# A fourth attention unit of each layer is turned by a DMA transpose: its words laid apart by GpSimd, joined one step later, its value products one step later

## The chip, the cores and the metric

The kernel runs on one core of one Trainium2 chip. The metric is device time in microseconds. Before the change the median of three runs is 1626.21 us (1625.96 to 1626.82).

## The reference, cut to what matters

A decoder trunk of two layers runs over 512 tokens of width 1024, all in float32. Each layer is a SwiGLU block, a mixing block and a second SwiGLU block. The mixing block holds the attention that the change touches:

```
z = rms_norm(x) @ W_in -> q (8 heads of 64), k, v (2 heads of 64), conv_B, conv_C, conv_h
scores = q @ k^T / 8 + ALiBi bias      window of 128: each block of 128 queries sees
                                       its own block of keys and the one before
p   = exp(scores - m) / (sum + exp(sink - m))
att = p @ v                            per head
y   = conv_B * depthwise_conv3(conv_C * conv_h)
x   = x + concat([att, y]) @ W_out
```

## The kernel before, in words

**Products.** Every matrix product is made of three TensorE passes over float32r halves: a number is split into a high part and the rest, and hi·hi, hi·lo and lo·hi are summed. A weight block is therefore loaded ("raw", 512 KB, line 210), cast on ScalarE to "wh", and subtracted on VectorE to "wl" (both line 228). The block `need_split` keeps two such splits ahead of TensorE. One group of 24 matmuls (lines 318, 319, 321) makes one 128 by 512 result "acc".

**The mixing block as steps.** `mix` runs the 18 groups of W_in in a fixed order. After the groups that make the queries and the convolution's inputs, a function `attend(step)` puts in a piece of attention: steps 6 to 17 each follow one group (`go_on`). A step's group and pieces stand in one instruction stream per engine. A planner orders each stream by the order of the program and by when it thinks that operands are ready, and the chip then works through each stream strictly in order.

**Attention units.** There are eight units, numbered 0 to 7: four blocks of 128 queries for each of two key heads, with four query heads in each. Unit 5 is block 1 of the second key head, unit 6 block 2, unit 7 block 3. A unit passes through three stages, at the steps that three tables name (`SCORES_AT`, `TURN_AT`, `VALUES_AT`):

- `scores`: matmuls of q and k, the maximum on VectorE (line 1558), the exponential on ScalarE (1575), the division on VectorE (1583). The result "p" (128 by 4 by 256, float32) lies in a buffer of the same eight that hold raw weight blocks.
- `turn`: p must stand the other way round for the product with v. In units 0, 2, 4, 6 and 7 TensorE transposes it in 128 by 128 blocks into PSUM ("pt", line 1616; eight blocks for units 2, 6 and 7). ScalarE then casts each half to "ph" (1621) and VectorE subtracts to get "pl" (1622).
- `values`: four matmuls with v into "o" (1633, 1634), a copy of the lower half on ScalarE ("ol", 1636) and two additions on VectorE into the attention output "m" (1639).

**Three units go another way.** `SEND_AT = {7: 1, 9: 3, 11: 5}` says that units 1, 3 and 5 are turned by DMA. `send` copies p on ScalarE so that the upper and the lower 16 bits of all words lie apart in a room called "crossing" (line 1590), and a DMA transpose from the queue of SyncE writes them, turned, back into p's buffer (1592). Two steps later `turn` calls `join` instead of the TensorE transposes: two ScalarE copies (line 1601) put the halves of the words together again, into the same room. The casts and subtractions follow as in the other units. The room has two places, used in turn: units 1 and 5 use the first, unit 3 the second.

**What sets the order around the change.** Three things. First, `attend` returns the last subtraction of the step's `turn`, and `go_on` then asks for the next weight splits under `tc.issue_after(last.ins)`: on VectorE the subtraction that makes "wl" may not stand ahead of that instruction. At step 14 the last instruction is that of unit 6, and two splits are asked for there. Second, the loads of W_out (ten blocks, four of them with a second load from GpSimd's queue that adds to the first, line 223) need raw buffers, and these come free when the units' p buffers and earlier splits are done with. Third, at step 17 the output projection begins (lines 827): its first chain "x_m" takes the tokens 0 to 255, and its third chain needs "ft2", sums over the tokens 0 to 511 that VectorE makes from m (lines 601, 602, then the split of line 228). GpSimd's own work here is two elementwise operations per convolution group (lines 1715, 1716) and the adding loads.

Of the kernel before, what the change touches and what calls it, by code (L numbers as in the profile page):

```python
# [54 lines left out]
STREAM_BACK_AT = {9: 0, 11: 1, 16: 2, 18: 3}  # L55
SCORES_AT = (5, 6, 7, 8, 9, 10, 12, 13)

SEND_AT = {7: 1, 9: 3, 11: 5}
TURN_AT = (6, 9, 8, 11, 10, 13, 14, 15)
VALUES_AT = (7, 10, 9, 12, 11, 14, 15, 16)  # L60
INSIDE = (11, 4, 5)
WARM = 3
XT_TAGS = ("sc", "aux", "aux", "mm", "sc", "sc", "aux", "aux")
# [12 lines left out]
def trunk_kernel(  # L76
# [23 lines left out]
    nc = tc.nc  # L100
# [34 lines left out]
    def words(ap):  # L135

        return ap.bitcast(U16).rearrange("p (n two) -> p two n", two=2)
# [1356 lines left out]
    def mix(l, norm, after):  # L1494
# [40 lines left out]
        class Unit:  # L1535
# [49 lines left out]
            def send(self):  # L1585


                self.room = crossing[:, todo.index(self) // 2 % 2, :]
                halves = self.room.bitcast(U16).rearrange("p (two n) -> p two n", two=2)
                nc.scalar.copy(halves, words(self.p.rearrange("p h k -> p (h k)")))  # L1590
                self.turned = self.p.rearrange("p h k -> p (h k)").bitcast(U16)
                nc.sync.dma_start_transpose(
                    self.turned.rearrange("p (c q) -> p c q", q=P),
                    halves.rearrange("p two n -> p (two n)"),
                )
# [11 lines left out]
            def turn(self):  # L1607

                self.pt = []
                for kb in range(self.lo // P, 2):  # L1610
                    if todo.index(self) in SEND_AT.values():
                        tp = self.join(kb)
# [30 lines left out]
        todo = [Unit(n, g) for g in range(NKV) for n in range(NT)]  # L1643
        crossing = g8(f"crossing_{l}", F32, (P, 2, 4 * 2 * P))

        def attend(step):

            done = None
            if step in SEND_AT:
                todo[SEND_AT[step]].send()  # L1650
            for at, stage in ((VALUES_AT, "values"), (TURN_AT, "turn"), (SCORES_AT, "scores")):
                if stage == "turn" and step + 1 == INSIDE[0]:
                    done = todo[VALUES_AT.index(step)].added
                    continue
                if step in at:
                    done = getattr(todo[at.index(step)], stage)() or done
            return done

        for j in range(NH // 2):
            acc = group(norm.h) if j else qacc  # L1660
            if j == 3:
                vv = take_values()
            qf = scaled(acc, f"qf_{l}_{j}", by=1.0 / 8.0)
            both = form(f"q_{l}_{j}", shape=(P, 2, S))
            qe, qo = both[:, 0, :], both[:, 1, :]
            nc.scalar.copy(qe[:HD, :], qf[:HD, :])
            nc.scalar.copy(qo[HD:, :], qf[HD:, :])
            nc.vector.tensor_sub(qe[HD:, :], qf[:HD, :], f32(qe[:HD, :]))
            nc.vector.tensor_sub(qo[:HD, :], qf[HD:, :], f32(qo[HD:, :]))
            q[2 * j], q[2 * j + 1] = qe, qo  # L1670
            attend(2 + j)
# [4 lines left out]
        step = 6  # L1676

        def product():

            def between(k, hi, lo):  # L1680
                if step == INSIDE[0] and k == INSIDE[2]:
                    todo[INSIDE[1]].turn()

            return group(norm.h, between, own=take_split(SPLIT_AHEAD - 1))

        def go_on():

            nonlocal step
            last = attend(step)
            if step == TURN_AT[-1]:  # L1690
                state["turned"] = last.ins
            step += 1
            with tc.issue_after(last.ins) if last else nullcontext():
                need_split(state["group"] - 1 + SPLIT_AHEAD + (step >= TURN_AT[-1]))

        for pair in range(2):
# [22 lines left out]
            for j in range(2):  # L1719
                last = nc.vector.tensor_mul(mixed[1][:, 2 * pair + j, :], product(), ys[j])  # L1720
# [64 lines left out]
```

## Time and profile before

| quantity | value |
|---|---|
| median of the runs shown | 1626.21 us |
| profiled execution: its time | 1626.19 us |
| profiled execution: its span | 1624.4 us |
| granted TensorE clock | 0.999 |
| TensorE matmul busy | 1615.4 us (99%) |
| VectorE busy | 1376.7 us (85%) |
| ScalarE busy | 1178.1 us (73%) |
| GpSimd busy | 216.5 us (13%) |

Shares are of the whole span. The steps that the change touches lie near 417 to 470 us in the first layer and near 1220 to 1273 us in the second, so a share over the span says little about them; the rows of those stretches do. "PE" is TensorE, "DVE" VectorE, "ACT" ScalarE, "POOL" GpSimd, and "SP" the queue of SyncE that issues most DMAs. In the lists by time a row gives start, duration, engine, line, operation and tiles, and in square brackets how long the engine had sat idle before and what ended that.

### The profile page before, as it was taken

Reading aid. Unit: us, or ns where it says so; the run is one execution under the profiler, and the core shown is the slowest. Engines: PE = TensorE matmul, PEld = TensorE weight load, DVE = VectorE, ACT = ScalarE, POOL = GpSimd, SP = SyncE. Lnnn points to the kernel's source line nnn. Section 1 sums busy time; section 2 is a strip of 40 time slices with the busy share of each in tenths; the row PEclk is TensorE's granted clock in tenths of the full one; section 3 lists DMA queues with packets and bytes.
Section 4 is the critical chain, followed back from the end, with each engine's and each line's share of the span. In section 5 each row is a group of like instructions: output and inputs, shape, how many; then the busy total and the mean of one; then the engine's idle time right before and its main releaser. Section 6 shows DMA issues by size and latency. Waiting matters only on the chain.

```text
span 1624.4 us, 21158 instructions
## 1 busy us (share of the span) xinstructions
PE 1615.4 (99%) x7571; PEld 1349.4 (83%) x7571; DVE 1376.7 (85%) x1788; ACT 1178.1 (73%) x1511; POOL 216.5 (13%) x191
## 2 busy tenths in 40 slices
PE   9999999999999999999999999999999999999998
PEld 7888888888898888888888888888888988888887
DVE  7978798988899977798998777989688998678997
ACT  6677777857766677778866777788586767878665
POOL 1211111001211111111011111110012111111121
PEclk9999999999999999999999999999999999999999
DMA  9999989822597698999767999998136978999892
GB/s 270 212 232 209 220 207 226 233 59 78 143 227 175 177 225 214 218 214 225 218 144 182 224 215 226 215 221 217 42 91 156 233 149 219 225 223 222 241 230 72
DMA packets 306031, 313.92 MB, mean 193 GB/s; under 512 B 125501, under 2 KB 188549, under 8 KB 305925
## 3 DMA queue, kind: packets, MB, share of 16 engines
q1 hardware_dynamic: 265412, 230.90, 50.1%
q0 software_dynamic: 40048, 81.27, 29.3%
q8 instruction: 59, 0.97, 0.2%
q14 instruction: 48, 0.39, 0.1%
q10 hardware_dynamic: 464, 0.40, 0.1%
HBM read 264.29 MB, written 2.10 MB: 164 GB/s over the span
## 4 chain that ended last, share of the span: by engine, by line
PE 98%; DVE 1%; DMA 0%; SPq 0%; issue 0%; ACT 0%; DVEq 0%
PE x L842 27%; PE y L842 13%; PE x_s L842 9%; PE acc L318 7%; PE acc L319 7%; PE acc L321 7%; PE w L842 7%; PE y_s L842 5%; PE x_m L827 3%; PE w_s L842 3%; PE y_m L827 1%; PE y_e L842 1%; PE acc L699 1%; PE x_e L842 1%; PE w_m L827 1%; PE sc L1555 0%
## 5 line engine op out<-in xcount | busy, mean ns | idle before, releaser
L228 DVE TENSOR_TENSOR wl<-raw,wh 128x1024 fp32r<-128x1024 f32 (+1 forms) x494 | 598.6, 1219 | 162.8 <-ACT wh L228 161.9
L228 ACT CAST wh<-raw 128x1024 fp32r<-128x1024 f32 (+1 forms) x494 | 514.1, 1044 | 304.6 <-PE x L842 92.8
L318 PE MATMUL acc<-xh,wh 128*128 128x512 f32 x392 | 153.3, 393 | 0.5 <-ACT wh L228 0.5
L319 PE MATMUL acc<-xl,wh 128*128 128x512 f32 x392 | 153.1, 391 | 0.0
L321 PE MATMUL acc<-xh,wl 128*128 128x512 f32 x384 | 149.7, 390 | 0.0
L223 POOL DMA_DIRECT2D raw<-in_ffn_wu_dram x40 | 50.6, 1272 | 381.6 <-DMA raw<-in_ffn_wu_dram 268.6
L318 PEld LDWEIGHTS acc<-xh,wh 128*128 128x128 f32 x392 | 73.8, 188 | 15.0 <-ACT wh L228 0.6
L319 PEld LDWEIGHTS acc<-xl,wh 128*128 128x128 f32 x392 | 73.7, 188 | 14.5
L321 PEld LDWEIGHTS acc<-xh,wl 128*128 128x128 f32 x384 | 72.1, 188 | 15.3
L223 POOL DMA_DIRECT2D raw<-in_ffn_wd_dram x34 | 41.0, 1218 | 272.0 <-DMA raw<-in_ffn_wd_dram 122.3
L223 POOL DMA_DIRECT2D raw<-in_ffn_wg_dram x40 | 49.1, 1237 | 201.9 <-DMA raw<-in_ffn_wu_dram 84.7
L269 DVE TENSOR_TENSOR raw<-raw,raw 128x1024 f32<-128x1024 f32 x58 | 70.5, 1220 | 1.7 <-DMA raw<-in_ffn_wu_dram 1.2
L1106 ACT COPY raw_a<-turned 128x1024 uint16<-128x1024 uint16 x48 | 63.5, 1357 | 0.0
L842 PE MATMUL x<-wl,ft1h 128*128 128x512 f32 x160 | 62.4, 390 | 0.0
L842 PE MATMUL w<-wh,fb21h 128*128 128x512 f32 x160 | 62.3, 390 | 0.0
L842 PE MATMUL y<-wh,ft3h 128*128 128x512 f32 x160 | 62.3, 390 | 0.0
L842 PE MATMUL x<-wh,ft1l 128*128 128x512 f32 x160 | 62.3, 389 | 0.0
L842 PE MATMUL x<-wl,ft2h 128*128 128x512 f32 x160 | 62.3, 389 | 0.0
L842 PE MATMUL x<-wh,ft2l 128*128 128x512 f32 x160 | 62.3, 389 | 0.0
L842 PE MATMUL x<-wh,ft1h 128*128 128x512 f32 x160 | 62.3, 389 | 0.0
L842 PE MATMUL w<-wh,fb21l 128*128 128x512 f32 x160 | 62.2, 389 | 0.0
L842 PE MATMUL y<-wh,ft3l 128*128 128x512 f32 x160 | 62.2, 389 | 0.0
(517 smaller groups left out, 4545.2 us busy)
## 6 DMA issues: line engine op xcount, KB each, us to landing
raw<-in_ffn_wu_dram SPq DMA_DIRECT2D x127, 512.0 KB, 5.6
raw<-in_ffn_wd_dram SPq DMA_DIRECT2D x105, 512.0 KB, 5.6
raw<-in_ffn_wg_dram SPq DMA_DIRECT2D x86, 512.0 KB, 5.3
raw<-in_ffn_wu_dram POOLq DMA_DIRECT2D x40, 512.0 KB, 9.1
raw<-in_ffn_wg_dram POOLq DMA_DIRECT2D x40, 512.0 KB, 6.5
raw<-in_w_in_dram SPq DMA_DIRECT2D x36, 512.0 KB, 4.0
raw<-in_ffn_wd_dram POOLq DMA_DIRECT2D x34, 512.0 KB, 8.2
raw<-in_w_out_dram SPq DMA_DIRECT2D x20, 512.0 KB, 4.6
```

Source lines behind the costliest of these rows:

```text
L223: nc.gpsimd.dma_start(out=r, in_=rows_of(*more), accum_op=ALU.add)
L228: return nc.scalar.copy(hi, raw), eng.tensor_sub(lo, raw, f32(hi))
L269: nc.vector.tensor_add(a11, a11, s1)
L318: nc.tensor.matmul(acc, hi[:, k, :], rhs[k][0], start=k == first, stop=False)
L319: nc.tensor.matmul(acc, hi[:, k, :], rhs[k][1], start=False, stop=False)
L321: nc.tensor.matmul(acc, lo[:, k, :], rhs[k][0], start=False, stop=k == last)
L699: nc.tensor.matmul(opening[n], (lo if part == "w" else hi)[:, k, :], xl if part == "x" else xh, start=n not in begun, stop=k == KC - 1 and ...
L827: nc.tensor.matmul(accs[c // 2][:, c % 2, :], w[:, k, cols], x_[:, 2 * h + k, :], start=start and c % 2 == 0 and h + k + i == 0, stop=h + ...
L842: nc.tensor.matmul(accs[u], x_[:, 2 * h + k, tok], w[:, k, :], start=start and h + k + i == 0, stop=h + k == 2 and i == 2, skip_group_chec ...
L1106: nc.scalar.copy(words(raws[self.b][:, c, :]), self.to[:, :, c, :])
```

## The change

Unit 6 joins the units that are turned by DMA. It is sent at step 13, and its `turn` stays at step 14, so one step lies between the two and not two. Its `values` move from step 15 to step 16, where unit 7's also are. The copy that lays its words apart is put on GpSimd (`IDLE_LAYS`), not on ScalarE. It uses the second place of the crossing room, after unit 3.

In `attend` a step may now hold several units of one stage, and the instruction that unit 6's `turn` returns is no longer handed on: at step 14 nothing is returned, so the two weight splits asked for there are no longer queued behind it.

```diff
-SEND_AT = {7: 1, 9: 3, 11: 5}
+SEND_AT = {7: 1, 9: 3, 11: 5, 13: 6}
 TURN_AT = (6, 9, 8, 11, 10, 13, 14, 15)
-VALUES_AT = (7, 10, 9, 12, 11, 14, 15, 16)
+VALUES_AT = (7, 10, 9, 12, 11, 14, 16, 16)
+IDLE_LAYS = (6,)
...
-                nc.scalar.copy(halves, words(self.p.rearrange("p h k -> p (h k)")))
+                lay = nc.gpsimd.tensor_copy if todo.index(self) in IDLE_LAYS else nc.scalar.copy
+                lay(halves, words(self.p.rearrange("p h k -> p (h k)")))
...
-                if step in at:
-                    done = getattr(todo[at.index(step)], stage)() or done
+                for n in (n for n, when in enumerate(at) if when == step):
+                    last = getattr(todo[n], stage)()
+                    done = done if n in IDLE_LAYS else last or done
```

## The prediction

> **What bounds the kernel now.** I read the page first, then the chain of waits in the two mixing blocks, then each engine's list by time from step 12 to the output projection.
>
> ```profile
> PE 1615.4 (99%) x7571; PEld 1349.4 (83%) x7571; DVE 1376.7 (85%) x1788; ACT 1178.1 (73%) x1511; POOL 216.5 (13%) x191
> ...
> PE 98%; DVE 1%; DMA 0%; SPq 0%; issue 0%; ACT 0%; DVEq 0%
> ```
>
> TensorE has work all the time, and the chain that ended last runs through it for 98%. So an instruction taken from TensorE is a gain, if nothing else becomes late. The chain of the first and of the second layer:
>
> ```profile
> 431.39 0.87 PE pt L1616 x8
> ...
> 438.66 0.87 PE pt L1616 x8
> ...
> 451.61 5.75 PE x_m L827 x48
> 457.36 5.76 PE w_m L827 x48
> 463.12 5.89 PE x_m L827 x48
> ```
>
> ```profile
> 1234.12 0.87 PE pt L1616 x8
> ...
> 1254.10 5.75 PE x_m L827 x48
> ...
> 1265.61 5.94 PE x_m L827 x48
> ```
>
> The reader is to see two things. Unit 6's eight transposes hold the chain for 0.87 us in each layer (unit 7's follow at 438.66). And of the first three chains of the output projection, 48 matmuls each, the third takes 0.13 and 0.18 us longer than the others: its operand ft2l comes just late, and that is VectorE's. Its load around that place, in the first layer:
>
> ```profile
> 445.00:450.00 5.00, 5.00 (x22) 3.93 (x22) 4.96 (x7) 1.43 (x2) 1.21 (x1) 1.00 0.92 315
> 450.00:455.00 5.00, 5.00 (x38) 4.73 (x37) 5.00 (x6) 2.67 (x3) 2.40 (x2) 1.00 0.57 95
> 455.00:460.00 5.00, 5.00 (x44) 5.00 (x43) 5.00 (x6) 3.38 (x4) 3.09 (x3) 1.00 1.11 206
> 460.00:465.00 5.00, 5.00 (x42) 4.92 (x42) 5.00 (x6) 3.83 (x4) 0.00 (x0) 1.00 1.15 202
> ```
>
> The columns are the stretch, its length, and the busy time of TensorE, weight loads, VectorE, ScalarE and GpSimd; then the granted clock, the DMA share and GB/s. VectorE is full from 445 to 465. So TensorE can reach the third chain earlier only if VectorE also does. VectorE's last free time before it:
>
> ```profile
> 426.49 1.14 DVE L1583 TENSOR_SCALAR p<-p,sums 128x256 f32<-128x256 f32 x4
> ...
> 427.54 0.68 DVE L1622 TENSOR_TENSOR pl<-crossing,ph 128x512 fp32r<-128x512 f32 x1
> ...
> 429.36 1.22 DVE L228 TENSOR_TENSOR wl<-raw,wh 128x1024 fp32r<-128x1024 f32 x1
> ...
> 432.90 0.16 DVE L1579 TENSOR_TENSOR sums<-sums,es 128x4 f32<-128x4 f32 x1 [1.45 <-ACT es L1578]
> ...
> 435.90 1.44 DVE L1622 TENSOR_TENSOR pl<-pt,ph 128x512 fp32r<-128x512 f32 x2
> 437.25 3.46 DVE L228 TENSOR_TENSOR wl<-raw,wh 128x1024 fp32r<-128x1024 f32 x2
> 440.63 0.68 DVE L1707 TENSOR_TENSOR ch<-acc,cc 128x512 f32<-128x512 f32 x1
> 442.72 0.75 DVE L1712 SCALAR_TENSOR_TENSOR tap<-ch,par,tap 128x510 f32<-128x510 f32 x1 [1.41 <-ACT tap L1711]
> ```
>
> There are two gaps, 1.45 us before 432.90 and 1.41 us before 442.72. Unit 6's pair "pl" (435.90) and behind it the two weight splits (437.25) stand between them.
>
> **The change part by part.**
>
> *TensorE.* The eight transposes go: -0.87 us a layer, -1.74 us in both. The value products of unit 6 only move a step. No other TensorE instruction is added.
>
> *The copy on GpSimd.* No copy of 2048 two-byte elements is in GpSimd's rows. The nearest are these:
>
> ```profile
> L173 POOL CAST ones_r<-ones 128x128 fp32r<-128x128 f32 x1 | 0.3, 288 | 0.0
> ...
> 434.85 1.22 POOL L223 DMA_DIRECT2D raw<-in_w_out_dram  x1 [32.02 <-ACT ol L1636]
> 435.63 1.77 POOL L1715 TENSOR_TENSOR cc<-cc,tap 128x511 f32<-128x511 f32 x1
> 437.48 2.15 POOL L1716 TENSOR_TENSOR cc<-cc,inv 128x512 f32<-128x512 f32 x1
> ...
> 444.92 1.29 POOL L1716 TENSOR_TENSOR cc<-cc,inv 128x512 f32<-128x512 f32 x1
> ```
>
> The one-input cast takes 288 ns for 128 elements, 2.25 ns each at most. Taking off about 0.1 us that is not per element (an estimate), it is some 1.5 ns, so 2048 make 3.1 us. Upper bound: 2.15 us for 512 with a busy VectorE, 8.6 us. Lower bound: two elements at a time, 1.6 us. I take 3.1 us, since the cast has one input as the copy has. Unit 6's p is ready at 427.6 (its division, 426.49 and 1.14), GpSimd stands idle for 32 us until 434.85, so the copy ends at 431 to 432.
>
> What it costs VectorE: L1716 takes 1.29 us at 444.92 but 2.15 us at 437.48, and the two "wl" take 3.46 us, not twice 1.22. That is +0.86 and +1.02. In those rows the later one of each pair seems to wait for the whole of the other. The copy would so hold up the "wl" of 429.36, which ends at 430.6, until 431 to 432.5. I take +1.9 us on VectorE's order, with 0.5 as the other end, if they only share.
>
> The Trainium skill, "SBUF — State Buffer", section "Who interferes with whom", says that a VectorE instruction with two SBUF inputs and a GpSimd instruction that reads SBUF exclude each other for the whole instruction. With plain sharing the sum would come out near 1624.3 us, with exclusion at the value below. These rows side with exclusion.
>
> *VectorE's order.* Unit 6's pair "pl" (1.44 us) leaves its place, and one of the two splits (1.22 us), no longer queued behind it, can go into the 1.45 us gap. Together -2.66 us against +1.9 us, so "ch" of step 15 comes some 0.7 us earlier. If ph is there by then, the moved pair fits the second gap of 1.41 us at no cost. VectorE then reaches ft2l 0.7 us earlier, and TensorE keeps about 0.6 of its 0.87 us. If not, the pair costs its 1.4 us behind the gap and VectorE is 0.7 us late. The additions of unit 6 (line 1639) lie after the gap in both kernels.
>
> *Transpose and join.*
>
> ```profile
> L1592 SPq DMA_TRANSPOSE p<-crossing x6: 1567/1613/1627, 385.0 to 1218.1; - x6
> ...
> DMA to landing us min/median/max: 3.6/3.7/5.2
> ```
>
> ```profile
> L1601 ACT COPY crossing<-p x12: 1339/1359/1373, 388.9 to 1223.0; 128x1024 uint16<-128x1024 uint16 x12
> ```
>
> ```profile
> 420.66 2.57 ACT L1601 COPY crossing<-p 128x1024 uint16<-128x1024 uint16 x2 [2.40 <-DMA p<-crossing]
> ...
> 434.59 0.59 ACT L1621 CAST ph<-pt 128x512 fp32r<-128x512 f32 x1
> ...
> 441.35 0.72 ACT L1709 ACTIVATE cc<-ch,par 128x512 f32<-128x512 f32 x1 [2.74 <-DVE ch L1707]
> ```
>
> From 432 the transpose lands at 435.6 to 437.2. The join adds 2.57 us to ScalarE, and the casts stay. ScalarE has 2.74 us free before 441.35, which cover it; without that cover it costs 2.57 us ahead of unit 7's casts. ph is then ready at about 440 to 441, so pl falls into VectorE's second gap, if narrowly. TensorE now wants it near 443: the group of step 16 began at 439.5, behind unit 7's transposes, and begins some 1.8 us earlier (0.87 for the transposes, 0.9 for the moved values); its 24 matmuls of 512 columns take about as long as a chain's 48 of 256, some 5.5 us. Behind a late join stand, on ScalarE, the copies of line 1709 and 1711 and unit 7's casts, and for those VectorE and then values(7) wait.
>
> *SP's and GpSimd's queues.* p's buffer comes free at the end of the join and not after the transposes of TensorE. A load of W_out waits for it:
>
> ```profile
> SPq L210 <- PE pt L1616: 1.3, 1, 1.3
> ```
>
> ```profile
> 430.64 2.02 SPq L210 DMA_DIRECT2D raw<-in_w_out_dram  x2
> ...
> 438.56 0.37 SPq L210 DMA_DIRECT2D raw<-in_w_out_dram  x1
> ...
> 439.57 1.21 POOL L223 DMA_DIRECT2D raw<-in_w_out_dram  x1
> ```
>
> ```profile
> raw<-in_w_out_dram SPq DMA_DIRECT2D x20, 512.0 KB, 4.6
> ```
>
> ```profile
> L269 DVE TENSOR_TENSOR raw<-raw,raw x2: 1215/1216/1218, 451.0 to 452.7; 128x1024 f32<-128x1024 f32 x2
> ```
>
> The second load of the row at 430.64 is that one; GpSimd adds to it at 439.57. The planner will give it the next buffer, free near 438, some 5 to 6 us later. With 4.6 us to land it is there near 442.6, and the adding load is issued 3 us later than before. VectorE wants the sum at 452.7, for the third chain. The transpose itself stands in SP's order near 431; a load behind it waits a microsecond or two, for blocks that are wanted after 451. I cost both at nothing.
>
> *Sum.* Per layer -0.6 us, two layers -1.2 us. Against the profiled execution (1626.19 us, 1.79 us over its span of 1624.4; 0.02 us under the median) this gives **1625.0 us**. The likeliest case's own range is 1624.1 (all 1.74 us and the 0.31 us of the late ft2l) to 1625.9.
>
> **The rivals.**
>
> *The gain is eaten by VectorE.* The pair pl misses the gap. For it speaks that ph comes at 440 to 441 at best, and that the row at 420.66 shows a join waiting 2.40 us for its transpose with two steps between; against it, that the split is free to move. VectorE is 0.7 us late, TensorE loses that: +0.6 us a layer, **1627.4 us**.
>
> *Slower: the delayed load stops VectorE.* If GpSimd's adding load is put behind lines 1715 and 1716 of step 15, which wait for "tap" (442.72), it is issued at about 446, not 439.57. With the 8.1 us that the old one took to land it comes at 454, and VectorE, strictly in order at line 269 and without free time after, waits about 2 us. That is paid in the third chain, in both layers: +4.2 us, **1630.4 us**. It decides when the issue falls after 444.6 (452.7 less 8.1). For it speaks the buffer's later release; against it, that the planner could also put line 269 later.
>
> ```profile
> DMA to landing us min/median/max: 8.1/8.1/8.1
> ```
>
> *The join blocks ScalarE.* If the planner thinks the transpose lands 2.4 us before it does, as at 420.66, and puts the join ahead of line 1709 of step 14, ScalarE stands still from about 433 to 436, and all behind it comes 3 to 5 us later, of which the gaps take 2.7 us: about 1 us a layer over no gain, **1628.5 us**; from 1.6 us a layer it is measurably slower.
>
> **How the numbers follow.** A difference of 0.2% (3.25 us) is about what a measurement of this kernel can tell from no change. All of TensorE's gain is 1.74 us, 0.11%, so the forecast and the first rival both count as no change. Chances: forecast 0.45, eaten 0.25, delayed load 0.16, join 0.11, and 0.03 for more than 3.25 us gained, which would need a stall removed that I don't see. Slower takes all of the delayed load and under half of the join: 0.20. The range goes from 1624.0 to the delayed load's 1630.4.
>
> **What would show it.** Right: no "pt" of eight between steps 14 and 15, a GpSimd copy of about 3 us, a "wl" near it stretched, pl<-crossing in VectorE's gap before "tap", and the third x_m near 5.75 us. Wrong: o matmuls (1633, 1634) or x_m with longer spacing, a wait of VectorE at line 269 for a DMA, ScalarE idle behind "DMA p<-crossing" for more than 2.7 us, or a copy beyond 5 us.

## The result and the profile after

The changed kernel takes 1633.89 us (median of 6, 1632.69 to 1634.54) against 1626.41 us (1625.96 to 1627.02) for the kernel before: ratio 1.0045, interval 1.0032 to 1.0058. It is 7.5 us slower, above the range of 1624.0 to 1630.4 us. The profiled execution took 1632.69 us, with a span of 1630.9 us, 6.5 us above the one of before. In the changed kernel most line numbers of the mixing block are 1 to 3 higher: the pair "pl" is line 1624, the convolution's GpSimd operations are 1718 and 1719, the adding loads 224, the split 229.

First the page of the changed kernel, busy times and shares of the chain of waits:

```profile
PE 1617.0 (99%) x7555; PEld 1348.8 (83%) x7555; DVE 1383.4 (85%) x1788; ACT 1182.0 (72%) x1515; POOL 221.0 (14%) x193
...
PE 94%; DVE 4%; ACT 1%; issue 1%; DMA 0%; SPq 0%; DVEq 0%
```

TensorE has 16 matmuls fewer and is nevertheless busy for longer, and VectorE's share of the chain has risen from 1% to 4%. The chain in time, first and second layer (start, duration, what):

```profile
438.00 4.52 DVE pl L1624 x2
...
451.67 2.23 DVE fb11l_m L229
...
465.97 4.10 PE x_m L828 x32
```

```profile
1243.77 4.28 DVE pl L1624 x2
...
1272.10 3.98 PE x_m L828 x31
```

The last row of each begins with the matmul that takes up the second operand, ft2l, of the output projection's third product. In TensorE's list of before that matmul starts at 463.11 and 1265.65; now it starts at 465.97 and 1272.10. That is 2.9 us later in the first layer and 6.5 us later after both, so the whole loss lies in these two stretches. Between the first and the last row of each, the chain has no piece of TensorE: it runs over VectorE and, for its copies, ScalarE. VectorE's list by time shows what stands there:

```profile
429.14 1.70 DVE L229 TENSOR_TENSOR wl<-raw,wh 128x1024 fp32r<-128x1024 f32 x1
430.84 1.21 DVE L229 TENSOR_TENSOR wl<-raw,wh 128x1024 fp32r<-128x1024 f32 x1
432.65 1.21 DVE L229 TENSOR_TENSOR wl<-raw,wh 128x1024 fp32r<-128x1024 f32 x1
...
435.23 0.75 DVE L1715 SCALAR_TENSOR_TENSOR tap<-ch,par,tap 128x510 f32<-128x510 f32 x1
...
438.00 4.52 DVE L1624 TENSOR_TENSOR pl<-crossing,ph 128x512 fp32r<-128x512 f32 x2 [1.27 <-ACT ph L1623]
442.45 0.68 DVE L1710 TENSOR_TENSOR ch<-acc,cc 128x512 f32<-128x512 f32 x1
...
449.86 1.81 DVE L229 TENSOR_TENSOR wl<-raw,wh 128x1024 fp32r<-128x1024 f32 x1
451.60 2.31 DVE L229 TENSOR_TENSOR fb11l_m<-m,fb11h_m 128x1024 fp32r<-128x1024 f32 x1
```

Unit 6's pair takes 4.52 us, where it took 1.44 us before; "ch" of step 15 follows at 442.45 and not at 440.63. Later "fb11l_m" takes 2.31 us for a shape that otherwise takes 1.22. GpSimd's list by time for the same stretch:

```profile
427.54 2.22 POOL L1592 COPY crossing<-p 128x2048 uint16<-128x2048 uint16 x1 [24.89 <-DVE p L1584]
436.92 1.22 POOL L224 DMA_DIRECT2D raw<-in_w_out_dram  x1 [7.16 <-DVE m L1641]
437.71 1.76 POOL L1718 TENSOR_TENSOR cc<-cc,tap 128x511 f32<-128x511 f32 x1
...
439.74 2.23 POOL L1719 TENSOR_TENSOR cc<-cc,inv 128x512 f32<-128x512 f32 x1
448.06 1.20 POOL L224 DMA_DIRECT2D raw<-in_w_out_dram  x1 [6.09 <-DMA raw<-in_w_out_dram]
448.84 1.74 POOL L1718 TENSOR_TENSOR cc<-cc,tap 128x511 f32<-128x511 f32 x1
450.65 2.16 POOL L1719 TENSOR_TENSOR cc<-cc,inv 128x512 f32<-128x512 f32 x1
```

Two collisions can be read off.

*The first.* The convolution's operations of step 14 began at 435.63 before, behind an adding load that started at 434.85. They stand behind that load now too, but it starts 2.07 us later, at 436.92. What it waits for is, by the times, the first load, to which it adds: in both kernels it starts 0.6 us after that one has landed. (The rows name ScalarE's "ol" before and VectorE's "m" now, which end near the same moment.) The first load was issued at 430.64 and took 3.6 us; now it is issued at 431.49, right behind the new DMA transpose in SyncE's queue, and takes 4.8 us. So the operations stand at 437.71 and 439.74, beside the pair pl (438.00). The two engines' operations alternate: line 1718 ends at 439.47, then the first pl at about 440.03, then line 1719 at 441.97, then the second pl at 442.5.

*The second.* The third adding load, which before stood behind the operations of step 15, now stands ahead of them and waits 6.09 us for the load that it adds to. The operations behind it start at 448.84, and meet the split at 449.86 and fb11l_m.

For a line, the profile gives the shortest, median and longest operation in ns, first and last start:

```profile
L1624 DVE TENSOR_TENSOR pl<-crossing,ph x16: 662/832/2572, 400.3 to 1245.5; 128x512 fp32r<-128x512 f32 x16
L1624 DVE TENSOR_TENSOR pl<-pt,ph x12: 679/684/693, 377.8 to 1251.3; 128x512 fp32r<-128x512 f32 x12
```

The same subtraction never takes more than 693 ns when its first operand is "pt", in PSUM; when it is the crossing room, in SBUF, it takes up to 2572 ns. Before, unit 6's pair was of the first kind, and its place beside GpSimd's operations cost it next to nothing.

What it costs TensorE stands in its list by time and in its waits (total us, times, longest):

```profile
443.53 0.39 PE L1636 MATMUL o<-pl,vv 128*128 128x512 f32 x1
445.16 0.50 PE L1635 MATMUL o<-ph,vv 128*128 128x512 f32 x1 [1.24 <-ACT ph L1623]
...
447.12 0.63 PE L319 MATMUL acc<-xh,wh 128*128 128x512 f32 x1
447.55 0.63 PE L320 MATMUL acc<-xl,wh 128*128 128x512 f32 x1
```

```profile
PE o L1635 <- ACT ph L1623: 2.2, 2, 1.2
PE x_m L828 <- DVE fb11l_m L229: 2.0, 1, 2.0
...
PE o L1636 <- DVE pl L1624: 0.6, 2, 0.3
...
PE x_m L828 <- DVE ft2l_m L229: 0.5, 2, 0.2
```

The way from pl to TensorE is a chain over three engines: the pair is late, so ch is late; ScalarE's copies wait for ch, unit 7's casts ph stand behind these copies, and the value products of unit 7 wait for ph. (Those of unit 6, from 442.85 on, wait for nothing.) Between 443.53 and 445.16 TensorE starts no matmul, where it otherwise starts one every 0.23 us.

The matmuls from 447.12 on show a second loss of TensorE: they start 0.43 us apart and wait for nothing. By stretches of time (length, busy times, then the granted clock):

```profile
440.00:446.00 6.00, 4.49 (x20) 3.17 (x18) 4.60 (x6) 3.13 (x6) 1.97 (x2) 1.00 1.02 233
446.00:447.00 1.00, 1.00 (x3) 0.70 (x4) 1.00 (x2) 0.98 (x2) 0.00 (x0) 0.78 1.18 242
447.00:450.00 3.00, 3.00 (x8) 2.32 (x8) 2.93 (x7) 0.73 (x2) 1.94 (x2) 0.51 0.96 221
```

The clock that TensorE was granted fell to about half behind the wait. The loss is 0.22 · 1.00 + 0.49 · 3.00 = 1.7 us of full clock. It happened in the first layer only; in the second the same wait was followed by full clock, but there TensorE waited 2.0 us for fb11l_m. That the slow clock made the kernel any longer isn't shown: TensorE took up fb11l_m at 454.04, when it had just been finished (453.91), and the layer with the slow clock lost 2.9 us, the one without it 3.6.

### The profile page after: what moved, and what is told of

It reads as the page before. It is cut to its first block, busy times and chain, and to the rows that moved or that the text cites. A ratio compares the mean times of both kernels' runs of the same rounds, so it can differ in the third digit from the quotient of the medians.

```text
span 1630.9 us, 21139 instructions
## 1 busy us (share of the span) xinstructions
PE 1617.0 (99%) x7555; PEld 1348.8 (83%) x7555; DVE 1383.4 (85%) x1788; ACT 1182.0 (72%) x1515; POOL 221.0 (14%) x193
## 4 chain that ended last, share of the span: by engine, by line
PE 94%; DVE 4%; ACT 1%; issue 1%; DMA 0%; SPq 0%; DVEq 0%
PE x L843 27%; PE y L843 13%; PE x_s L843 9%; PE w L843 7%; PE acc L319 7%; PE acc L320 7%; PE acc L322 6%; PE y_s L843 5%; PE w_s L843 3%; PE x_m L828 2%; PE y_m L828 1%; PE y_e L843 1%; DVE wl L229 1%; PE acc L700 1%; PE x_e L843 1%
## 5 line engine op out<-in xcount | busy, mean ns | idle before, releaser
L843 PE MATMUL x<-wl,fb11h 128*128 128x512 f32 x160 | 62.2, 389 | 0.0
L843 PE MATMUL w<-wl,fb21h 128*128 128x512 f32 x160 | 62.2, 389 | 0.0
```

The source lines that it names most:

```text
L843: nc.tensor.matmul(accs[u], x_[:, 2 * h + k, tok], w[:, k, :], start=start and h + k + i == 0, stop=h + k == 2 and i == 2, skip_group_chec ...
```

## The experiments

My theory after the result: the pair pl, now with two operands in SBUF, and GpSimd's operations exclude each other, and they meet because of the order of GpSimd's queue. The rivals: GpSimd's new copy is the cause; the move of the values and the freed splits are; or the DMA transposes themselves (their packets, the load behind them) are. Every run is told with its ratio to the kernel before on the same chip; a time alone differs by a few tenths of a us from chip to chip.

**GpSimd's operations of step 14 left out.**

```diff
+                if c not in (2,):
-                nc.gpsimd.tensor_add(y[:, 1:], y[:, 1:], tap[:, 1:])
-                nc.gpsimd.tensor_mul(y, y, norm.inv)
+                    nc.gpsimd.tensor_add(y[:, 1:], y[:, 1:], tap[:, 1:])
+                    nc.gpsimd.tensor_mul(y, y, norm.inv)
```

> The changed kernel with GpSimd's two elementwise operations of the convolution group of step 14 (in the changed kernel lines 1718 and 1719, near 438 to 442 us) left out, so that group's result is not the reference's. Theory C (collision): unit 6's two subtractions into pl now read two SBUF operands and wait for exactly these two GpSimd operations; without them the pair takes 1.3 to 1.5 us and not 4.5, the next ch comes 2.5 to 3 us earlier, and the time falls by about 3 us a layer, to 1626 to 1629 us. Rival L (lateness): ph of unit 6 comes too late, with only one step between send and turn; pl still starts near 438, TensorE still waits, and the time stays above 1632 us.

Measured: 1630.49 us, ratio 1.0025 (1.0014 to 1.0035). Its lists of VectorE and of GpSimd by time:

```profile
438.43 0.69 DVE L1624 TENSOR_TENSOR pl<-crossing,ph 128x512 fp32r<-128x512 f32 x1 [1.27 <-ACT ph L1623]
439.83 0.69 DVE L1624 TENSOR_TENSOR pl<-crossing,ph 128x512 fp32r<-128x512 f32 x1 [0.71 <-ACT ph L1623]
440.44 0.69 DVE L1710 TENSOR_TENSOR ch<-acc,cc 128x512 f32<-128x512 f32 x1
...
448.99 3.15 DVE L229 TENSOR_TENSOR fb11l_m<-m,fb11h_m 128x1024 fp32r<-128x1024 f32 x1
```

```profile
448.54 1.20 POOL L224 DMA_DIRECT2D raw<-in_w_out_dram  x1 [8.65 <-DMA raw<-in_w_out_dram]
```

Without GpSimd's operations the pair takes twice 0.69 us, in time that VectorE has free ahead of ch, and ch starts at 440.44, 0.2 us earlier than in the kernel before. So the pair does what the theory said. The time doesn't: it lies above the 1626 to 1629 us expected, though below the rival's 1632. Under half of the loss goes; what stays is the second collision, with fb11l_m at 3.15 us.

**The same operations and those of step 15 left out.** As above with `if c not in (2, 3)`.

> The changed kernel with GpSimd's elementwise operations of the convolution groups of steps 14 and 15 left out in both layers, so that half of the convolution is not the reference's. Theory C2: nothing is left for VectorE to collide with in these steps but the copy; 1624 to 1626.5 us. Rival L2: 1628 us or more, with TensorE waiting for pl of unit 6 or for the splits behind it.

Measured: 1624.56 us, ratio 0.9989 (0.9980 to 0.9998), as expected. With both collisions away the kernel is a little faster than before. Here work is missing, so this shows the causes and is no version to use.

**The join copied into PSUM for the pair.**

```diff
+                if todo.index(self) in IDLE_LAYS:
+                    tp = psum("aux", [P, 4 * P], f"joined_{self.name}_{kb}")
+                    nc.scalar.copy(tp, whole)
+                    whole = tp
```

> The changed kernel with one more ScalarE copy per half in unit 6: the joined words are copied to PSUM, and ph and pl are made from there, so that the subtraction reads one SBUF operand. Theory C: pl of unit 6 takes 1.4 us although GpSimd works beside it; ScalarE has 1.2 us more a layer; time 1627 to 1630 us. Rival L: the way from p to pl is longer by 1.2 us, so TensorE waits longer, 1634 to 1637 us.

Measured: 1631.52 us, ratio 1.0034 (1.0021 to 1.0047).

```profile
439.61 2.24 POOL L1723 TENSOR_TENSOR cc<-cc,inv 128x512 f32<-128x512 f32 x1
```

```profile
439.33 0.69 DVE L1628 TENSOR_TENSOR pl<-joined,ph 128x512 fp32r<-128x512 f32 x1 [2.35 <-ACT ph L1627]
```

The operand's place decides the duration: 0.69 us in PSUM while one of GpSimd's operations runs beside it. For the time the run is inconclusive (it lies between the two ranges named), because the added copies make ph later and the planner ordered the rest otherwise.

**The copy on ScalarE.** `lay = nc.scalar.copy` for unit 6 too.

> The changed kernel with unit 6's words laid apart by ScalarE (1.9 us) as in the other units, and not by GpSimd. Rival G (the copy on GpSimd holds up VectorE's weight split near 429 us, and that is what is lost): 1627 us or less. Theory C: the copy costs VectorE 0.5 us at that place only, and the collision at 438 us stays; ScalarE has 1.9 us more; 1632 to 1637 us.

Measured: 1632.43 us, ratio 1.0038 (1.0024 to 1.0052). The loss stays, as theory C expected, and so do both collisions (3.83 us for the pair, 2.28 for fb11l_m). So GpSimd's copy isn't its cause.

**The copy alone, in the kernel before.** Nobody reads what it writes.

```diff
+            if step == 13:
+                spare = crossing[:, 1, :].bitcast(U16).rearrange("p (two n) -> p two n", two=2)
+                nc.gpsimd.tensor_copy(spare, words(todo[6].p.rearrange("p h k -> p (h k)")))
```

> The kernel before with one GpSimd copy added a layer: unit 6's p is laid apart at step 13 into the free second place of the crossing room, and nobody reads it. It prices the copy by itself. Measured beside the change it takes 2.2 us and stretches one weight split on VectorE from 1.22 to 1.70 us. If that is all, the time is within 0.7 us of the kernel before; if the lock on VectorE reaches the end, 1627.5 us or more.

Measured: 1627.52 us, ratio 1.0006 (0.9997 to 1.0016). The copy costs one split 0.5 us (1.70 us for 1.22). The median is 1.2 us above the 1626.34 us of the kernel before on the same chip: more than the 0.7 us that I expected, and just at the rival's 1627.5. TensorE also waits 0.4 us for unit 7's pl in the first layer, which it didn't before. But the interval takes in no change, so it stays open whether the copy alone costs time. The whole loss (0.45%) it can't be.

**Unit 6 turned by TensorE again, the other edits kept.**

```diff
-SEND_AT = {7: 1, 9: 3, 11: 5, 13: 6}
+SEND_AT = {7: 1, 9: 3, 11: 5}
```

> The changed kernel without the transpose by DMA: unit 6 is turned by TensorE as before, its values stay at step 16 beside unit 7's, and the two weight splits of step 14 stay free of it. Theory C: pl of unit 6 reads PSUM, nothing collides that did not before, 1625 to 1628 us. Rival T (the values of two units at one step, or the freed splits, make the loss): 1631 us or more.

Measured: 1625.71 us, ratio 0.9994 (0.9985 to 1.0004). Moved values and freed splits aren't the cause either. Unit 6's pair reads PSUM here. GpSimd's operations still meet a split, and fb11l_m takes 2.31 us as in the changed kernel, but it ends at 445.56 and TensorE waits for nothing in this stretch: a collision costs time only where its result is late.

**The splits queued behind unit 6's pair again.** `done = last or done` in place of the line with `IDLE_LAYS`.

> The changed kernel with unit 6's last subtraction handed on, so that the two weight splits of step 14 are queued behind it on VectorE again, as in the kernel before. Theory: freeing the splits is worth 1.2 us or more a layer on VectorE, since they now fill its gap near 432; without it they follow pl near 442 us and the time rises to 1637 to 1642 us. Rival (the freed splits themselves do the harm, by leaving pl to GpSimd's operations): 1628 us or less.

Measured: 1638.76 us, ratio 1.0073 (1.0058 to 1.0088): 0.28% (4.6 us) more than the changed kernel. So the freed splits do help; what they are worth by themselves this run doesn't say. A part of the 4.6 us is the clock's. In the profiled execution it fell in both layers, in the first behind 3 us in which TensorE was busy for 1.25 (0.56 of the clock for the next 7 us, a loss of 3.1 us of full clock against 1.7 in the changed kernel), and here the chain of waits runs through the slow matmuls:

```profile
441.00:448.00 7.00, 6.02 (x14) 4.54 (x15) 5.60 (x8) 3.32 (x6) 2.73 (x3) 0.56 1.07 340
```

**The adding loads queued behind GpSimd's operations.** Nothing is left out; only the order of GpSimd's queue changes.

```diff
+                with tc.issue_after(state["conv"]) if state["conv"] else nullcontext():
-                nc.gpsimd.dma_start(out=r, in_=rows_of(*more), accum_op=ALU.add)
+                    nc.gpsimd.dma_start(out=r, in_=rows_of(*more), accum_op=ALU.add)
...
-                nc.gpsimd.tensor_mul(y, y, norm.inv)
+                state["conv"] = nc.gpsimd.tensor_mul(y, y, norm.inv).ins
...
+        state["conv"] = None
```

> The changed kernel with GpSimd's adding loads of W_out (line 224 there) queued behind the two elementwise operations of the last convolution group traced; nothing else differs. Theory C2: the loss has two collisions, both because an adding load that waits for its first load stands ahead of the elementwise operations on GpSimd and shifts them: those of step 14 (from 435.6 to 437.7 us) into unit 6's pl, those of step 15 (from 443.6 to 448.8 us) into the splits wl and fb11l. With the order put right, the step 14 pair runs near 436 to 438.7 and meets at most the first pl (0.7 us lost and not 3.1), the step 15 pair runs by 446, fb11l takes 1.2 us; time 1625 to 1628 us. Rival L2 (once the collisions are gone, the late ph of unit 6 still holds VectorE): 1629 to 1631 us.

Measured: 1624.82 us, ratio 0.9988 (0.9979 to 0.9998). The whole loss is gone, and a gain of 0.12% is left, a little more than expected. The DMA transposes are all still there, so by themselves they aren't the cause. GpSimd and VectorE by time:

```profile
436.46 1.29 POOL L1719 TENSOR_TENSOR cc<-cc,tap 128x511 f32<-128x511 f32 x1 [6.35 <-DVE tap L1716]
437.82 1.31 POOL L1720 TENSOR_TENSOR cc<-cc,inv 128x512 f32<-128x512 f32 x1
```

```profile
438.37 2.09 DVE L1625 TENSOR_TENSOR pl<-crossing,ph 128x512 fp32r<-128x512 f32 x2 [1.29 <-ACT ph L1624]
...
449.08 1.22 DVE L230 TENSOR_TENSOR fb11l_m<-m,fb11h_m 128x1024 fp32r<-128x1024 f32 x1
```

GpSimd's operations now start as soon as their operand "tap" is there. The pair takes 2.09 us and not 4.52, and fb11l_m its 1.22.

**The same order in the kernel before.** The three edits above, applied to it.

> The kernel before, with the same queue order as in the run whose adding loads stand behind the convolution's two GpSimd operations. If that order only mends what the change has upset (my theory), it does next to nothing here: 1626.0 to 1626.9 us, since in the kernel before the convolution's operations do not meet a pair pl that reads the crossing room. Rival: the order is the whole gain by itself, whatever the units do; then this kernel comes to about 1624.8 us as well.

Measured: 1626.05 us, ratio 0.9998 (0.9989 to 1.0008). That is as expected. The order is worth nothing there: it mends what the change upset.

**The order at step 14 alone, and at step 15 alone.** The instruction is noted only for `c == 2`, or only for `c == 3`.

> The changed kernel, with the adding loads queued behind the convolution's GpSimd operations of step 14 only. If the two collisions are apart, the first (pl at 438 us, 4.5 us for two) goes and the second (the adding load that waits for its first load ahead of the operations of step 15, and fb11l_m beside them) stays: about 1630 us, as where the operations of step 14 were left out (1630.5). Rival: all of the loss hangs on the first collision; then about 1625 us.

Measured: 1626.47 us, ratio 1.0003 (0.9994 to 1.0013).

> The changed kernel, with the adding loads queued behind the convolution's GpSimd operations of step 15 only. The first collision stays, with 3 us more for the pair pl in each layer, the second goes. If the two add up: 1628 to 1631 us. Rival: the second alone decides, since VectorE makes up for the first by the time the output projection wants its operands; then about 1625 us.

Measured: 1629.00 us, ratio 1.0016 (1.0007 to 1.0026). GpSimd in the first of the two, VectorE in the second:

```profile
444.32 1.20 POOL L225 DMA_DIRECT2D raw<-in_w_out_dram  x1 [2.62 <-PE o L1636]
445.07 1.77 POOL L1719 TENSOR_TENSOR cc<-cc,tap 128x511 f32<-128x511 f32 x1
```

```profile
438.45 4.30 DVE L1625 TENSOR_TENSOR pl<-crossing,ph 128x512 fp32r<-128x512 f32 x2 [1.31 <-ACT ph L1624]
```

The two collisions don't add up. Against the changed kernel, mending the first takes 0.42% off, mending the second 0.29%, mending both 0.57%. My expectation for step 14 alone (about 1630 us) was wrong: with the first collision gone, the third adding load waited 2.62 us and not 6.09, and the operations behind it were through before fb11l_m. They met an earlier split instead:

```profile
444.51 3.43 DVE L230 TENSOR_TENSOR wl<-raw,wh 128x1024 fp32r<-128x1024 f32 x1
```

So the second collision is moved and not gone: in this profiled execution (1627.64 us, where the ten lie between 1625.69 and 1628.87) fb11l_m comes behind that split, and TensorE waits 1.7 us for it. The adding load came earlier because its first load landed sooner. That load was issued at 438.47 here, and at 438.35 in the run that leaves step 14's operations out, but took 5.3 us and not 9.6. In five of the runs the first of step 14's adding loads started between 436.26 and 437.54, and there this load took 9.4 to 10.0 us; in the two in which the adding load started behind the operations, from 439.06 on, it took 5.3 and 5.7 us. That the loads slow each other is likely, and no run tests it by itself. For step 15 alone the expectation held: 4.30 us for the pair, and the loss of the values' wait.

**Unit 6 turned by TensorE, with the order.**

> Unit 6 turned by TensorE again, its values at step 16 and its splits free, with the adding loads behind the convolution's GpSimd operations: what the DMA transpose itself brings is this run less the run with the transpose and the same order (1624.8 us). If taking the eight transposes off TensorE is worth anything: 1625.5 to 1626.5 us. Rival: the gain of that run is the order and the free splits alone; then 1624.8 us here too.

Measured: 1625.65 us, ratio 0.9998 (0.9988 to 1.0007). The run with transposes by DMA and the same order had 0.9988. The difference, 0.10% or 1.6 us, is near the 1.74 us of TensorE's 16 transposes, but the intervals overlap, and in the run with TensorE's transposes VectorE waits 0.9 us for a load at the sum (line 271). So that it is the transposes that bring it is likely and not shown.

## Why the prediction was wrong, step by step

*TensorE.* The 16 transposes are gone, and where VectorE let it TensorE came out ahead: with the order mended, the third product goes on with its second operand at 462.37, against 463.11 before (TensorE's lists of both):

```profile
463.11 0.39 PE L827 MATMUL x_m<-ft2l_m,wh 128*128 128x256 f32 x1
...
462.37 0.38 PE L829 MATMUL x_m<-ft2l_m,wh 128*128 128x256 f32 x1
```

That is 0.74 us in the first layer and 1.51 us after both, and 0.6 a layer was forecast. The time of that kernel, 1624.82 us, lies near the forecast of 1625.0 us. So the mechanism of the gain agrees with that run; it is not what decided.

*The copy on GpSimd.* Forecast 3.1 us with bounds of 1.6 and 8.6, measured 2.22. That is 1.08 ns an element, not the 1.5 that I had scaled from a cast of 128 elements; so small an operation is a poor scale. (The 0.1 us taken off there fits GpSimd's one-element fills (memset) in the kernel before, 96 to 102 ns.) The forecast also misadded: a copy of 3.1 us from 427.6 ends at 430.7, not at 431 to 432; it ended at 429.76. The cost to VectorE was 0.5 us (1.70 us for a split), the low end of 0.5 to 1.9. It was ready earlier and met less of the split.

*VectorE's order.* Both splits that were freed went ahead, to 430.84 and 432.65, where one was counted. **The step that failed is the next one: "Unit 6's pair pl (1.44 us) leaves its place" and "fits the second gap of 1.41 us at no cost".** The 1.44 us came from the row pl<-pt, which reads PSUM. The moved pair reads the crossing room. I had set out the exclusion two paragraphs above, for the copy and the split, and didn't apply it to the one VectorE instruction whose operand the change moves into SBUF. The Trainium skill, "SBUF — State Buffer", section "Who interferes with whom", says that at most one SBUF input, outside VectorE's two-port modes, means no contention and two mean contention with a GpSimd instruction that reads SBUF; the runs agree (0.69 us from PSUM beside running operations, up to 2.57 us from SBUF beside them, 0.69 us from SBUF beside none). With two operations of 1.29 us to wait for (the row of before at 444.92), the pair could have cost up to 1.44 + 2 · 1.29 = 4.0 us, against 4.52 and 4.28 measured. The place was wrong as well. The pair doesn't lie in the second gap: it stands ahead of "ch" (438.00 and 442.45), in the room that the two splits left, and the second gap is still there, empty (1.40 us before "tap" at 444.53). So what holds up the pair holds up ch and all that waits for it.

*Transpose and join.* They were earlier than forecast. The queue of SP and ScalarE by time, changed kernel:

```profile
429.79 1.60 SPq L1594 DMA_TRANSPOSE p<-crossing  x1
431.49 16.23 SPq L211 DMA_DIRECT2D raw<-in_w_out_dram  x6
```

```profile
434.85 2.58 ACT L1603 COPY crossing<-p 128x1024 uint16<-128x1024 uint16 x2
437.27 0.63 ACT L1623 CAST ph<-crossing 128x512 fp32r<-128x512 f32 x1
...
438.73 0.64 ACT L1623 CAST ph<-crossing 128x512 fp32r<-128x512 f32 x1
```

The transpose was issued directly behind the copy; the join did not wait for it, and ph was made from 437.27 to 439.37 where I said 440 to 441. So lateness of ph is not what failed: in the run without GpSimd's operations of step 14 the pair, made from a ph just as late, held up nothing. The rival that the join blocks ScalarE is out: unit 6's join waits for the transpose in neither layer.

*SP's and GpSimd's queues.* "I cost both at nothing" is the second half of the failed step. Both queues carried the loss, through what is queued behind an adding load and not through the load itself. The prediction had counted that a load behind the transpose waits "a microsecond or two, for blocks that are wanted after 451". But an adding load waits for that load, and the convolution's operations wait behind the adding load. At step 14 it started 2.07 us later than before (the first of the six loads above is the one that it adds to) and held the convolution's operations from 435.98, when "tap" was there (435.23 and 0.75), to 437.71, beside the pair. At step 15 one waited 6.09 us. The rival of the delayed load had seen that this queue would set the time, but with the order the wrong way round: it put the load behind the operations, with VectorE waiting at the sum of the two loads. The planner put the operations behind the load, at step 14 in both kernels and at step 15 in the changed one; the sum (now line 270) waited for nothing, and placing the loads behind the operations is what mended it.

*The sum.* Forecast 0.6 us gained a layer; measured 2.9 and 3.6 us lost. Of the terms, waits of TensorE for ph, pl, fb11l_m and ft2l_m make 5.3 us by the profile's own count, and the clock 1.7 us, both over both layers, against 1.74 us saved. The rest, about 1.2 us, is in the slower starts of the matmuls behind each wait, which that count leaves out. This is a count of where TensorE's time went; what set the end of each stretch is VectorE, as the chain shows, so the clock's 1.7 us isn't shown to be a cause of its own.

*What would show it.* The signs I named for "wrong" did show: value products and x_m with longer spacing. The chain of waits then named VectorE's pl. My first rival had pl late by 0.7 us a layer, because of a late ph; none had it held up by GpSimd.

## What to carry to other kernels

When a change moves an operand from PSUM into SBUF, price every VectorE instruction that reads it again: beside GpSimd's elementwise work a 0.69 us subtraction took up to 2.57 us. A DMA that waits at the head of an in-order queue delays the compute behind it; here that decided 9 us, and putting the loads behind the compute in GpSimd's queue cost the kernel before nothing that could be measured. When a moved step lands in a gap, look at what GpSimd does in that gap, after the change and not before it.

## What the runs showed of the hardware that I had not expected

The granted clock of TensorE fell to about half for some 3.4 us (0.22/0.49 of the first microsecond and 3.0 us at 0.51) behind a stretch in which TensorE was busy for 4.49 of 6.00 us, with no single wait over 1.24 us. In the run with step 15's order alone TensorE was busy for 4.86 us of the same 6.00, and the clock stayed full:

```profile
440.00:446.00 6.00, 4.86 (x21) 3.46 (x19) 4.60 (x5) 3.36 (x6) 2.61 (x3) 1.00 1.06 238
446.00:447.00 1.00, 0.83 (x3) 0.53 (x4) 1.00 (x3) 0.97 (x2) 0.92 (x2) 1.00 1.10 262
```

The Trainium skill, "TensorE: Matmul & The Clock Gate", section "What's actually happening", describes two states, half and full, and free-running windows of about 3.4 us. The depth and the length agree with the trace; that an idle window of 3.4 us is needed for the fall does not, since the longest wait here was 1.24 us. What sets the fall off is not settled by these runs. The length of a wait alone isn't it: in the second layer of the changed kernel TensorE waited 1.96 us for fb11l_m and was busy for 2.04 of 4.00 us (1258 to 1262), and the clock stayed full. So a wait can cost TensorE more than its own length, and need not.
